# Seven products of quarters for most of a short convolution's input projection

## The chip, the core and the metric

The kernel runs on one core of a Trainium2 chip. The metric is the device time of one execution in microseconds (us). The engines of the core work side by side, each through its own instructions in a fixed order: PE (TensorE: matrix products, with PEld for its weight loads), DVE (VectorE), ACT (ScalarE), POOL (GpSimd), and SP, whose queue issues most DMAs. They wait for each other through semaphores. Matrix products write to PSUM, which holds 8 banks of 128x512 f32; everything else lies in SBUF. POOL works on SBUF alone here.

## What is computed

The kernel computes a whole small decoder: layer 0 with attention, layer 1 with a short convolution, each followed by an MLP and a gated embedding. The change is in the convolution of layer 1, whose reference is:

```python
D_MODEL = 1024; SEQ = 512; CONV_WIDTH = 3
def short_conv(h, w_in, conv_w, w_out):
    D = h.shape[-1]
    proj = h @ w_in
    b_gate = proj[..., :D]
    c_gate = proj[..., D:2 * D]
    u = proj[..., 2 * D:]
    z = c_gate * u
    zc = lax.conv_general_dilated(
        z, conv_w[:, None, :].astype(z.dtype), window_strides=(1,),
        padding=[(CONV_WIDTH - 1, 0)],
        dimension_numbers=('NWC', 'WIO', 'NWC'),
        feature_group_count=D)
    return (b_gate * zc) @ w_out
```

Here `h` is the normed residual stream (512 tokens x 1024 channels) and `w_in` is 1024 x 3072. Everything is f32.

## The kernel before, in words

**Products in three parts.** PE is fed numbers of the type fp32r, which keep fewer bits than f32. So each f32 operand is held as a pair: `hi`, the value cast to fp32r by ACT, and `lo`, the remainder, which DVE (or POOL) computes as `src - hi`. `split` (L218 to L222) issues both: the cast is L221, the subtraction L222. `mm3` (L211 to L217) then makes one product of three matmuls, hi by hi, hi by lo and lo by hi (L213, L214, L215).

**Weights.** All weights are loaded in one planned order, `order`. A weight tile of 128x512 f32 (256 KB) lands in one of 14 `raw` buffers by a DMA of SP's queue (`fetch`, L118), is split into two of the 70 buffers called pages (`prepare`), and is then read by PE. `wide` asks for a tile and has the next 8 of the order prepared with it (`SOON`). In the MLP, which already uses seven products of quarters for its second matrix, `derive` makes four sums of weight quarters per pair on POOL (L130), and POOL also computes the `lo` of those sums (L222 on POOL).

**The convolution** (`conv`). The normed stream lies transposed in `hT` (hi and lo), as 8 blocks of 128 channels by 512 tokens. The three outputs `c`, `u` and `b` are made in blocks of 128 output channels, so 24 blocks in all; `project` makes one block in one PSUM bank: 8 input blocks by three matmuls of 128x512, 24 matmuls. The loop goes over channel pairs `i0 = 0, 2, 4, 6`. For each of the two blocks of a pair it makes c and u, ACT copies c out of PSUM (`cs`, L650), DVE multiplies (`z`, L651), then b is made, and the three taps follow: one product on ACT (L659), two multiply-adds on DVE (L662), the product with b on DVE (L666), and the split into `yh` (ACT) and `yl` (DVE). The first pair is done in halves of 256 tokens, because the last token blocks of `hT` come late from the layer before; its matmuls are 128x256. POOL has no part in the convolution before.

**What follows.** The output product (`co`, in `mixer_out`) sums over all eight `y` blocks for each of 4 token blocks and 2 column halves. It can start with y0 to y5 while the last blocks are finished.

**Order.** The order of instructions on each engine is set when the program is built, by a scheduler that moves instructions on PE, DVE, ACT and POOL by its own estimate of their readiness; on the chip each engine then goes through its list strictly in that order.

Of the kernel before, what the change touches and what calls it, by code (L numbers as in the profile page):

```python
# [15 lines left out]
P = 128  # L16
D = 1024
# [32 lines left out]


class Pair:

# [8 lines left out]
@with_exitstack  # L62
def trunk(ctx: ExitStack, tc, x, pT, g, wv, wqk, bf, wo, wci, cw, wco, wup, wdn, wpp, wpg, out):
    nc = tc.nc
# [9 lines left out]
    def page(name, dtype=F32):  # L74
        return pages.tile([P, S], dtype, tag="pg", name=name)
# [14 lines left out]
    loads, order, where, ready, fetched, begun = [], [], {}, {}, [], [0]  # L90
    derived = {}

    def plan(key, src):
        where[key] = len(order)
        order.append((key, len(loads)))
        loads.append(src)

    def plan_down(l, gr):

        at = {}  # L100
        for name, r, c in (("B11", 0, 0), ("B21", 1, 0), ("B12", 0, 1), ("B22", 1, 1)):
            for p in range(2):
                at[name, p] = len(loads)
                loads.append(wdn[l, c, 4 * gr + 2 * p + r])
        for i in STEPS:
            name = PRODUCTS[i][1]
            for p in range(2):
                where["dn", l, gr, name, p] = len(order)
                order.append((("dn", l, gr, name, p), at if name[0] == "T" else at[name, p]))
        derived[l, gr] = at  # L110

# [7 lines left out]

    def derive(l, gr):  # L120
        at = derived.pop((l, gr))
        fetch(max(at.values()) + 1)
        B = {key: fetched[n][:, :S] for key, n in at.items()}
        for p in range(2):
            for name, a, b in (("T1", "B12", "B11"), ("T3", "B22", "B12"), ("T2", "B22", "T1"),
                               ("T4", "B21", "T2")):
                t = page(f"{name}_{l}_{gr}_{p}")
                derived[l, gr, name, p] = t
                B[name, p] = t[:, :S]
                nc.gpsimd.tensor_tensor(out=B[name, p], in0=B[a, p], in1=B[b, p], op=ALU.subtract)  # L130

    def prepare(upto):
        while begun[0] < min(upto, len(order)):
            n = begun[0]
            begun[0] += 1
            key, at = order[n]
            if key[0] == "dn" and key[1:3] in derived:
                derive(*key[1:3])
# [20 lines left out]
    for l in range(2):  # L159
# [10 lines left out]
        else:  # L170
            for i in range(0, KT, 2):
                for s, key in enumerate((("cu", i), ("b", i), ("cu", i + 1))):
                    for j in range(4):
                        plan((*key, j), wci[3 * (i // 2) + s, j])
            for n in range(2):
# [31 lines left out]
    def need(*keys):  # L207
        while any(k in keys for _, k, _ in later):
            later.pop(0)[2]()
# [420 lines left out]
    def conv(hT):  # L630
# [13 lines left out]

        def gates(i, z, lo, hi):
            n = hi - lo
            c = project(("cu", i), 0, f"c{i}_{lo}", lo, hi)
            u = project(("cu", i), 1, f"u{i}_{lo}", lo, hi)
            cs = page(f"cs{i}_{lo}")
            nc.scalar.copy(cs[:, :n], c[:, :n])  # L650
            nc.vector.tensor_tensor(  # L651
                out=z[:, lo:hi], in0=u[:, :n], in1=cs[:, :n], op=ALU.mult
            )

        def finish(i, z, y, lo, hi):
            n = hi - lo
            b = project(("b", i - i % 2), i % 2, f"b{i}_{lo}", lo, hi)
            a = page(f"za{i}_{lo}")
# [8 lines left out]
            split(y.hi[:, lo:hi], y.lo[:, lo:hi], a[:, :n])  # L667

        for i0 in range(0, KT, 2):
            zs, both = [], []  # L670
            for i in (i0, i0 + 1):
                zs.append(page(f"z{i}"))
                both.append(Pair(page(f"yh{i}", F32R), page(f"yl{i}", F32R)))
            for lo, hi in ((0, 256), (256, 512)) if i0 == 0 else ((0, 512),):
                gates(i0, zs[0], lo, hi)
                finish(i0, zs[0], both[0], lo, hi)
                gates(i0 + 1, zs[1], lo, hi)
                need(*range(NB))
                finish(i0 + 1, zs[1], both[1], lo, hi)
            ys += both  # L680
# [225 lines left out]
def layout(x, p, norm_g, w_attn_in, b_forget, w_attn_out, w_conv_in, conv_w, w_conv_out,  # L906
# [22 lines left out]
    ci = np.stack([c[:, :, 0], u[:, :, 0], b[:, :, 0], b[:, :, 1], c[:, :, 1], u[:, :, 1]], axis=2)  # L929
    got["wci"] = tiles(ci.reshape(D, 3 * D), 2, 256)  # L930
    got["cw"] = np.asarray(conv_w)[0].reshape(3, KT, P).transpose(2, 1, 0)
# [25 lines left out]
```

## Time and profile before

| what | value |
|---|---|
| median of 3 runs | 1249.44 us (1249.13 to 1250.35) |
| the profiled execution's own time | 1248.93 us |
| its span in the trace | 1247.2 us |
| granted clock of PE, mean over the span | 0.998 |
| busy in the span: PE, DVE, ACT, POOL | 1221.6, 918.0, 612.6, 633.9 us |
| convolution, first c matmul to first co matmul | 662.32 to 796.55 us of the span |

A row of a group names the source line, the engine, the operation, the tile written and the tiles read, the shapes and the count; behind the first bar stand the busy time of the group (us) and the mean duration of one (ns); behind the second the idle time of the engine just before, with what ended it. A row of the timeline has the start (us from the span's start), the length (us), the engine, line and operation, and in square brackets the idle time before it. Instructions of one engine overlap a little in the trace: a row of four that lasts 2.49 us has starts 0.62 us apart although one lasts 0.69.

### The profile page before, as it was taken

How to read it: one execution, taken by the hardware profiler on the slowest of the kernel's cores; microseconds unless marked ns; L12 is line 12 of the kernel's file. 1: busy time of each engine (PE TensorE's matmuls, PEld its weight loads, DVE VectorE, ACT ScalarE, POOL GpSimd, SP SyncE). 2: the span in 40 equal slices, each digit the busy share in tenths (PEclk: the TensorE clock that was granted, in tenths of full speed). 3: DMA queues.
4: the chain of work that ended last, by engine and by line, in shares of the span. 5: the costliest groups of instructions: out<-in, count | busy, mean ns of one | idle time of the engine just before them, and what ended most of it. 6: DMA issues, size and time to landing. Idle time of an engine off the chain costs nothing.

```text
span 1247.2 us, 18012 instructions
## 1 busy us (share of the span) xinstructions
PE 1221.6 (98%) x5972; PEld 1023.2 (82%) x5972; DVE 918.0 (74%) x1402; ACT 612.6 (49%) x1309; POOL 633.9 (51%) x631
## 2 busy tenths in 40 slices
PE   7999999999999999999999999999999999999997
PEld 6888887887888888888789888889788888888876
DVE  5657878676789778989877444457778898779972
ACT  5456777546544543454555223333654345535451
POOL 2016667256878777775211000017777778778210
PEclk9999999999999999999999999999999999999999
DMA  7456564532343224428224232432422442236401
GB/s 256 147 159 166 152 157 115 186 116 78 100 135 110 80 82 135 136 74 277 76 83 133 68 100 90 148 119 69 131 63 78 135 135 94 67 110 190 148 18 51
DMA packets 85789, 148.68 MB, mean 119 GB/s; under 512 B 10112, under 2 KB 17328, under 8 KB 85696
## 3 DMA queue, kind: packets, MB, share of 16 engines
q1 hardware_dynamic: 85488, 147.27, 38.2%
q8 instruction: 47, 0.77, 0.3%
q14 instruction: 46, 0.38, 0.1%
q10 hardware_dynamic: 144, 0.26, 0.1%
q0 software_dynamic: 64, 0.00, 0.0%
HBM read 136.93 MB, written 6.37 MB: 115 GB/s over the span
## 4 chain that ended last, share of the span: by engine, by line
PE 69%; DVE 13%; POOL 5%; issue 5%; ACT 4%; DMA 3%; SPq 0%; DVEq 0%; POOLq 0%; ACTq 0%
DVE wl L222 6%; PE up L214 6%; PE up L215 6%; PE up L213 6%; PE dn L214 5%; PE dn L213 5%; PE dn L215 5%; PE pg L213 2%; PE pg L214 2%; PE pg L215 2%; PE qk L214 2%; PE qk L213 2%; PE qk L215 2%; POOL s L715 2%; ACT junk L244 2%
## 5 line engine op out<-in xcount | busy, mean ns | idle before, releaser
L222 DVE TENSOR_TENSOR wl<-raw,wh 128x512 fp32r<-128x512 f32 (+1 forms) x404 | 364.7, 953 | 25.3 <-ACT wh L221 24.3
L221 ACT CAST wh<-raw 128x512 fp32r<-128x512 f32 (+1 forms) x404 | 219.7, 619 | 9.5 <-DVE xd L295 5.0
L214 PE MATMUL up<-hTh,wl 128*128 128x512 f32 (+1 forms) x576 | 210.1, 365 | 0.0
L215 PE MATMUL up<-hTl,wh 128*128 128x512 f32 (+1 forms) x576 | 209.8, 366 | 0.0
L213 PE MATMUL up<-hTh,wh 128*128 128x512 f32 (+1 forms) x576 | 209.3, 366 | 0.0
L222 POOL TENSOR_TENSOR wl<-T,wh 128x512 fp32r<-128x512 f32 x112 | 161.0, 1469 | 35.7 <-ACT wh L221 32.0
L213 PEld LDWEIGHTS up<-hTh,wh 128*128 128x128 f32 x576 | 108.6, 189 | 17.7
L214 PEld LDWEIGHTS up<-hTh,wl 128*128 128x128 f32 x576 | 108.6, 189 | 17.6
L215 PEld LDWEIGHTS up<-hTl,wh 128*128 128x128 f32 x576 | 108.3, 189 | 17.5 <-DVE hTl L222 0.2
L747 DVE TENSOR_TENSOR acc<-dn,acc 128x512 f32<-128x512 f32 x168 | 107.3, 679 | 8.5 <-PE dn L215 8.5
L130 POOL TENSOR_TENSOR T<-raw,raw 128x512 f32<-128x512 f32 x56 | 87.8, 1579 | 36.2 <-DMA raw<-in_wdn 23.7
L701 ACT ACTIVATE r<-up 128x512 f32<-128x512 f32 (+1 forms) x72 | 38.7, 546 | 122.7 <-PE up L215 114.7
L130 POOL TENSOR_TENSOR T<-raw,T 128x512 f32<-128x512 f32 x56 | 90.9, 1623 | 2.2
L687 DVE TENSOR_TENSOR q<-r 128x512 f32<-128x512 f32 (+1 forms) x72 | 68.6, 959 | 28.8 <-ACT r L701 28.6
L236 POOL TENSOR_SCALAR cor_r_v<-cos,cos 128x1 f32<-128x1 f32 x4 | 1.6, 398 | 159.1 <-ACT junk L244 159.1
L221 ACT CAST A11h<-q 128x256 fp32r<-128x256 f32 x28 | 11.4, 407 | 102.0 <-DVE q L687 102.0
L221 ACT CAST wh<-T 128x512 fp32r<-128x512 f32 x112 | 61.2, 617 | 0.0
L213 PE MATMUL pg<-wh,hTh 128*128 128x512 f32 x128 | 50.9, 397 | 3.5 <-ACT hTh L221 3.3
L754 POOL TENSOR_TENSOR acc<-acc,acc 128x512 f32<-128x512 f32 x28 | 46.9, 1706 | 10.1 <-DVE acc L747 10.1
L213 PE MATMUL qk<-hTh,wh 128*128 128x512 f32 x128 | 51.1, 399 | 0.0
L215 PE MATMUL qk<-hTl,wh 128*128 128x512 f32 x128 | 50.9, 397 | 0.0
L214 PE MATMUL pg<-wh,hTl 128*128 128x512 f32 x128 | 50.3, 393 | 0.0
(234 smaller groups left out, 3082.5 us busy)
## 6 DMA issues: line engine op xcount, KB each, us to landing
raw<-in_wup SPq DMA_DIRECT2D x128, 256.0 KB, 2.9
raw<-in_wdn SPq DMA_DIRECT2D x128, 256.0 KB, 2.9
raw<-in_wci SPq DMA_DIRECT2D x48, 256.0 KB, 3.2
raw<-in_wqk SPq DMA_DIRECT2D x32, 256.0 KB, 3.4
raw<-in_wpg SPq DMA_DIRECT2D x32, 256.0 KB, 3.5
g<-in_g SPq DMA_DIRECT2D x22, 256.0 KB, 5.9
prl<-neg_c SPq DMA_DIRECT2D x16, 256.0 KB, 6.6
raw<-in_wo SPq DMA_DIRECT2D x16, 256.0 KB, 5.1
```

The costliest lines, as they stand in the source:

```text
L130: nc.gpsimd.tensor_tensor(out=B[name, p], in0=B[a, p], in1=B[b, p], op=ALU.subtract)
L213: nc.tensor.matmul(ps, a.hi, b.hi, start=start, stop=False)
L214: nc.tensor.matmul(ps, a.lo, b.hi, start=False, stop=False)
L215: nc.tensor.matmul(ps, a.hi, b.lo, start=False, stop=stop)
L221: nc.scalar.copy(hi, src)
L222: eng.tensor_tensor(out=lo, in0=src, in1=hi.bitcast(F32), op=ALU.subtract)
L244: nc.scalar.activation(junk, src, AF.Square, scale=D**-0.5, accum_out=ss)
L687: nc.vector.tensor_tensor(out=out, in0=r, in1=r, op=ALU.mult)
L701: nc.scalar.activation(r[:, :n], ps[:, :n], AF.Relu)
L715: sums = lambda out, a, b, op: nc.gpsimd.tensor_tensor(out=out, in0=a, in1=b, op=op)
L747: nc.vector.tensor_tensor(out=a, in0=banks[s], in1=a, op=ALU.add)
L754: nc.gpsimd.tensor_tensor(out=a, in0=a, in1=acc[i, s][:, :S], op=ALU.add)
```

## The change

For c and b of the channel pairs 2, 4 and 6 and for u of the pairs 4 and 6 (`SEVENS`, eight groups of two output blocks), the product of a 1024 x 256 piece of weights with the 1024 x 512 stream is cut into quarters (512 x 128 of weights, 512 x 256 of the stream) and made by seven products in place of eight, with the scheme that the MLP already uses. The three others (u of pair 2, and all of pair 0) stay as they are.

- The host lays the 36 weight tiles of the pairs 2, 4 and 6 out anew (`wcq`); in a group of seven each of its 4 tiles is one quarter. Their number and size stay.
- `plan_sums` generalizes the plan of the MLP's sums. For each group of seven, POOL makes four sums of quarters (S1, S2, S3, S4). The group then has seven forms to split in place of four: seven casts on ACT, five subtractions on DVE, two (S3 and S4, `ON_POOL`) on POOL.
- `sums_of_tokens` makes four sums T1 to T4 of the stream's quarters, once, for all groups: half of each (q = 0) on DVE, half (q = 1) on POOL, ten 128x512 instructions on each; then eight casts on ACT and eight subtractions on DVE.
- `sevens` makes the seven products: each 4 input blocks by three matmuls of 128x256, two products in one PSUM bank. One ACT copy and seven DVE additions of 128x256, each with one operand in PSUM, put the two output blocks together in two pages in SBUF.
- z and the product with b therefore read SBUF alone where c or b come from sevens. The order within a pair becomes u, c, b for both blocks, and both blocks' taps come after b.

```diff
+SEVENS = {(s, i) for i in (2, 4, 6) for s in "cub" if s != "u" or i > 2}
+QUARTERS = ("A11", "A12", "S2", "S1", "S3", "S4", "A22")
+ON_POOL = ('S3', 'S4')
...
+    def plan_sevens(key, srcs):
+        plan_sums(
+            key,
+            [(f,) for f in QUARTERS],
+            [((name,), src) for name, src in zip(("A11", "A12", "A21", "A22"), srcs)],
+            [
+                ((name,), (a,), (b,), op)
+                for name, a, b, op in (
+                    ("S1", "A21", "A22", ALU.add), ("S2", "S1", "A11", ALU.subtract),
+                    ("S3", "A11", "A21", ALU.subtract), ("S4", "A12", "S2", ALU.subtract),
+                )
+            ],
+        )
...
+    def derive(key):
+        at, sums = recipes.pop(key)
         fetch(max(at.values()) + 1)
+        B = {name: fetched[n][:, :S] for name, n in at.items()}
+        for name, a, b, op in sums:
+            t = page("_".join(str(u) for u in (*key, *name)))
+            derived[(*key, *name)] = t
+            B[name] = t[:, :S]
+            nc.gpsimd.tensor_tensor(out=B[name], in0=B[a], in1=B[b], op=op)
...
-            if isinstance(at, dict):
-                raw, eng, w = derived.pop(key[1:]), nc.gpsimd, S
+            if isinstance(at, tuple):
+                raw, w = derived.pop(key), S
+                eng = nc.gpsimd if key[0] == "dn" or key[-1] in ON_POOL else nc.vector
...
+        def sums_of_tokens():
+            for q, eng in ((0, nc.vector), (1, nc.gpsimd)):
+                cut = lambda h, t: hT.at(
+                    lambda u: u.bitcast(F32)[:, 4 * h + 2 * q : 4 * h + 2 * q + 2, 256 * t : 256 * t + 256]
+                )
+                B = {f"B{h + 1}{t + 1}": cut(h, t) for h in range(2) for t in range(2)}
+                full = {}
+                for name, a, b in (("T1", "B12", "B11"), ("T2", "B22", "T1"),
+                                   ("T3", "B22", "B12"), ("T4", "B21", "T2")):
+                    at = page(f"{name}f{q}")
+                    t = at[:, :S].rearrange("p (k c) -> p k c", k=2)
+                    tt = lambda out, x, y, op: eng.tensor_tensor(out=out, in0=x, in1=y, op=op)
+                    if b in full:
+                        tt(t, B[a].hi, full[b], ALU.subtract)
+                        tt(t, t, B[a].lo, ALU.add)
+                    else:
+                        rest = page(f"{name}r{q}")[:, :S].rearrange("p (k c) -> p k c", k=2)
+                        tt(t, B[a].hi, B[b].hi, ALU.subtract)
+                        tt(rest, B[a].lo, B[b].lo, ALU.subtract)
+                        tt(t, t, rest, ALU.add)
+                    full[name] = t
+                    T[name, q] = Pair(page(f"{name}h{q}", F32R), page(f"{name}l{q}", F32R))
+                    split(T[name, q].hi[:, :S], T[name, q].lo[:, :S], at[:, :S])
...
+        def sevens(key, name):
+            out = [page(f"{name}{e}") for e in range(2)]
+            L, R = slice(0, 256), slice(256, S)
+
+            def products(*pairs):
+                ps = bank(f"{name}_{pairs[0][0]}")
+                for (a, b), c in zip(pairs, (L, R)):
+                    for k in range(4):
+                        w = wide(*key, a).at(lambda u: u[:, k * P : (k + 1) * P])
+                        mm3(ps[:, c], w, second(b, k), k == 0, k == 3)
+                return ps
+
+            add = lambda out, x, y: nc.vector.tensor_tensor(out=out, in0=x, in1=y, op=ALU.add)
+            ps = products(("A11", "B11"), ("A12", "B21"))
+            u = page(f"{name}u")
+            u2, u34 = u[:, L], page(f"{name}v")
+            nc.scalar.copy(u2, ps[:, L])
+            add(out[0][:, L], ps[:, R], u2)
+            p65 = products(("S2", "T2"), ("S1", "T1"))
+            add(u2, p65[:, L], u2)
+            add(u34[:, R], p65[:, R], u2)
+            p73 = products(("S3", "T3"), ("S4", "B22"))
+            add(u34[:, L], p73[:, L], u2)
+            add(out[1][:, R], p65[:, R], u34[:, L])
+            add(out[0][:, R], p73[:, R], u34[:, R])
+            ps = products(("A22", "T4"))
+            add(out[1][:, L], ps[:, L], u34[:, L])
+            return out
...
         for i0 in range(0, KT, 2):
...
+            if i0 == 0:
+                for lo, hi in ((0, 256), (256, 512)):
...
+                        if e:
+                            need(*range(NB))
+                            if lo == 0:
+                                sums_of_tokens()
+                        b = project(("b", 0), e, f"b{e}_{lo}", lo, hi)
+                        taps_of(e, zs[e], both[e], b, lo, hi)
+            else:
+                got = {}
+                for name in "ucb":
+                    if (name, i0) in SEVENS:
+                        got[name] = [o[:, :S] for o in sevens((name, i0), f"{name}{i0}")]
...
+                    if name == "c":
+                        for e in range(2):
+                            times(zs[e][:, :S], got["c"][e], got["u"][e])
+                for e in range(2):
+                    taps_of(i0 + e, zs[e], both[e], got["b"][e], 0, S)
```

`taps_of` is the former `finish` without its `project`; `times` is the DVE product.

More of the change, by code (lines that the diff above doesn't have):

```diff
@@ L62, in trunk @@
 @with_exitstack
-def trunk(ctx: ExitStack, tc, x, pT, g, wv, wqk, bf, wo, wci, cw, wco, wup, wdn, wpp, wpg, out):
+def trunk(ctx: ExitStack, tc, x, pT, g, wv, wqk, bf, wo, wci, wcq, cw, wco, wup, wdn, wpp, wpg, out):
     nc = tc.nc
@@ L643, in project @@
             return ps
-        def gates(i, z, lo, hi):
-            n = hi - lo
[L647 to L657, printed above, removed]
+        T = {}
```

111 lines of the change are left out of this document (72 added, 39 removed).

## The prediction

> **What bounds the kernel now.** I read the page first, then the windows of two stretches, then the groups of each by shape, then the timeline.
>
> ```profile
> span 1247.2 us, 18012 instructions
> ...
> PE 1221.6 (98%) x5972; PEld 1023.2 (82%) x5972; DVE 918.0 (74%) x1402; ACT 612.6 (49%) x1309; POOL 633.9 (51%) x631
> ...
> PEclk9999999999999999999999999999999999999999
> ...
> PE 69%; DVE 13%; POOL 5%; issue 5%; ACT 4%; DMA 3%; SPq 0%; DVEq 0%; POOLq 0%; ACTq 0%
> ```
>
> PE is busy for 98% of the span at full granted clock and holds 69% of the chain of waits. The windows of an MLP stretch and of the convolution's full-width part say how close the others are:
>
> ```profile
> core 0: us, PE busy (x) PEld busy (x) DVE busy (x) ACT busy (x) POOL busy (x), PEclk, DMA share, GB/s
> 400.00:540.00 140.00, 140.00 (x619) 115.92 (x618) 113.08 (x138) 61.34 (x115) 108.69 (x85) 1.00 0.34 104
> 700.00:796.00 96.00, 96.00 (x425) 79.51 (x424) 40.14 (x63) 27.63 (x49) 0.00 (x0) 1.00 0.35 108
> ```
>
> In the convolution PE never pauses, DVE works 42% of the time and POOL not at all. In the MLP, which uses seven products already, DVE stands at 81% and POOL at 78%, and PE still never pauses. So in the convolution a microsecond less of matmuls is a microsecond gained, as long as DVE and POOL keep up.
>
> **What PE gains.** From the timeline, the first matmuls of c and of u in the half-width part, of the first full-width block, and of the output product:
>
> ```profile
> 662.32 0.28 PE L213 MATMUL c<-hTh,wh 128*128 128x256 f32 x1
> ...
> 665.19 0.28 PE L213 MATMUL u<-hTh,wh 128*128 128x256 f32 x1
> ...
> 698.61 0.40 PE L213 MATMUL c<-hTh,wh 128*128 128x512 f32 x1
> ...
> 796.55 0.39 PE L213 MATMUL co<-wh,yh 128*128 128x512 f32 x1
> ```
>
> 24 half-width matmuls take 2.87 us, 0.1196 each. The 18 full-width blocks of the pairs 2, 4 and 6 are 432 matmuls in 97.94 us, 0.2267 each; two halves cost 5% more than a whole. A group of two blocks is 48 x 0.2267 = 10.88 us now and 7 x 4 x 3 = 84 x 0.1196 = 10.05 us after: 0.83 us saved instead of an eighth, and 8 x 0.83 = 6.7 us in all. If PE alone set the pace it would end the convolution at 796.55 - 6.7 = 789.9.
>
> **What the others get.** DVE's prices without POOL (groups by shape, 662 to 800 us), then DVE's and POOL's in the MLP (400 to 540 us):
>
> ```profile
> L222 DVE TENSOR_TENSOR wl<-raw,wh 128x512 fp32r<-128x512 f32 x51 | 32.0, 685 | 0.0
> L651 DVE TENSOR_TENSOR z<-u,cs 128x256 f32<-128x256 f32 x4 | 1.7, 423 | 5.8 <-PE u L215 5.8
> L662 DVE SCALAR_TENSOR_TENSOR za<-z,taps,za 128x256 f32<-128x256 f32 x4 | 1.9, 483 | 1.2 <-ACT za L659 1.2
> ```
>
> ```profile
> L222 DVE TENSOR_TENSOR wl<-raw,wh 128x512 fp32r<-128x512 f32 x46 | 48.7, 1109 | 0.0
> L747 DVE TENSOR_TENSOR acc<-dn,acc 128x512 f32<-128x512 f32 x46 | 29.3, 679 | 1.0 <-PE dn L215 1.0
> L222 POOL TENSOR_TENSOR wl<-T,wh 128x512 fp32r<-128x512 f32 x28 | 41.3, 1505 | 8.8 <-ACT wh L221 7.5 <-PE dn L214 1.3
> L130 POOL TENSOR_TENSOR T<-raw,T 128x512 f32<-128x512 f32 x14 | 22.5, 1607 | 0.5
> ```
>
> The same subtraction of DVE takes 685 ns while POOL is idle and 1109 beside a POOL that is busy 78% of the time; an addition with one operand in PSUM (acc) takes 679 either way. So DVE instructions that read SBUF alone pay 0.42 us each for POOL's company, and those with a PSUM operand nothing. The timeline shows the extreme, both engines with SBUF work queued:
>
> ```profile
> 434.18 5.93 DVE L222 TENSOR_TENSOR wl<-raw,wh 128x512 fp32r<-128x512 f32 x4
> ...
> 430.58 1.33 POOL L130 TENSOR_TENSOR T<-raw,raw 128x512 f32<-128x512 f32 x1 [1.58 <-PE dn L215]
> ...
> 434.43 3.44 POOL L130 TENSOR_TENSOR T<-raw,T 128x512 f32<-128x512 f32 x2
> 437.83 3.44 POOL L130 TENSOR_TENSOR T<-raw,raw 128x512 f32<-128x512 f32 x2
> ```
>
> Here one DVE subtraction takes 1.48 us and one POOL sum 1.72. The Trainium skill, "SBUF — State Buffer", section "Who interferes with whom", has the reason: a DVE instruction with two SBUF inputs and a POOL instruction that reads SBUF exclude each other for the whole instruction. That rule speaks against this change, which gives both of them SBUF work at once; the two rows agree in direction, though 1.48 is less than a full 1.33 on top of 0.62.
>
> The change puts exactly this mix into a stretch where POOL was idle. How DVE goes through a pair today:
>
> ```profile
> 679.27 0.69 DVE L222 TENSOR_TENSOR hTl<-n0b_p,hTh 128x512 fp32r<-128x512 f32 x1 [1.03 <-ACT hTh L221]
> ...
> 760.23 1.54 DVE L662 SCALAR_TENSOR_TENSOR za<-z,taps,za 128x511 f32<-128x511 f32 x2 [0.79 <-ACT za L659]
> 764.11 0.69 DVE L666 TENSOR_TENSOR za<-b,za 128x512 f32<-128x512 f32 x1 [2.35 <-PE b L215]
> 765.55 0.69 DVE L222 TENSOR_TENSOR yl<-za,yh 128x512 fp32r<-128x512 f32 x1 [0.74 <-ACT yh L221]
> 766.16 2.49 DVE L222 TENSOR_TENSOR wl<-raw,wh 128x512 fp32r<-128x512 f32 x4
> ...
> 798.13 0.69 DVE L222 TENSOR_TENSOR yl<-za,yh 128x512 fp32r<-128x512 f32 x1 [0.69 <-ACT yh L221]
> ```
>
> Prices in a queue: an SBUF instruction 2.49 / 4 = 0.62, a multiply-add 1.54 / 2 = 0.77, a half-width addition 0.42, a wait for ACT's cast 0.72 (0.69 and 0.74). With them I go down DVE's built list from the last `hTl`, which ends at 680.0. Charged beside POOL: 0.42 more per SBUF instruction.
>
> - To z of block 1: a half-width `yl`, four weight splits, z: 0.42 + 2.5 + 0.42 = 3.3, to 683.3.
> - Token sums: 10 sums and 8 splits, 18 x 0.62 = 11.2; each of the first four splits waits for ACT's cast, 2.9. POOL makes its own ten sums in the first half, so ten pay the charge, 4.2. 18.3, to 701.6. The four splits of POOL's half stand in DVE's queue, and the rest of pair 0 behind them; PE meanwhile fills PSUM banks with its blocks and has the next two full-width blocks of u to make until 709.5, before it needs a T. I cost this at nothing for PE; without that cover it would be the 3 or 4 us by which T comes after 698.6.
> - Rest of pair 0: 6 multiply-adds of half width at 0.48, 8 others at 0.42, one split, three waits for ACT: 9.1, to 710.7.
> - Pair 2 (c and b by sevens): 11 splits, 2 z, 2 products with b, 2 `yl` = 17 x 0.62, 4 x 0.77, 14 additions x 0.42, two waits: 20.9. All 21 SBUF instructions pay: 8.8. 29.7, to 740.4.
> - Pair 4 (three sevens): 15 splits, so 21 x 0.62, 4 x 0.77, 21 x 0.42, two waits: 26.4; 25 pay: 10.5. 36.9, to 777.3.
> - Pair 6: with two more splits (of the output weights) 27.6. POOL has about 8 of its 18 instructions left, since it works a group ahead; 27 x 0.42 x 8/18 = 5.0. 32.6, to 809.9.
>
> PE needs 3 x 10.05 = 30.2 us for pair 4, and needed 32.7; DVE asks for 36.9. With 18 POOL instructions at about 1.55 us, 28 us, POOL is busy 76% of that, like the 78% behind the charge. So DVE becomes the bound in the pairs 4 and 6, and what goes late is the splits of the next group's weights, which stand between the additions and taps, and at the end `yl` of block 7.
>
> The end: 44 matmuls of the output product stand in PE's built order ahead of the first that reads the last `yl`, 44 x 0.2267 = 10.0 us. PE alone would be there at 789.9 + 10.0 = 799.9, DVE at 809.9. The same place in the number of matmuls is 796.55 + 10.0 = 806.5 now, where nothing waits (last `yl` done at 798.8). So 809.9 - 806.5 = +3.4 us, and everything behind moves by as much.
>
> Costed at nothing: the weight loads, 48 tiles before and after, in groups of four (DMA share 0.35); and ACT, with three casts and a short copy more per group:
>
> ```profile
> L221 ACT CAST wh<-raw 128x512 fp32r<-128x512 f32 x48 | 26.3, 619 | 0.0
> ```
>
> That is some 2.2 us of 10 on an engine that is busy 27.63 of 96; both are covered by waiting that these engines do today. The four quarter sums of the first group (c of pair 2) run on POOL before 680, where DVE still has pauses; if they have none, it is four charges, 1.7 us.
>
> **Sum.** Against the profiled execution's own 1248.93 us (1.7 more than its span, 0.5 under the median): 1248.93 + 3.4 = 1252.3 us.
>
> The charge is the unknown. From 680 on it is paid 10 + 21 + 25 + 12 = 68 times, so DVE ends at 781.3 + 68 x charge. Its bounds are 0 (685 ns without POOL) and 1.48 - 0.62 = 0.86 (the crowded stretch). I take 0.42, the mean of a stretch where POOL is as busy. Up to 0.27 the whole 6.7 us are gained; at 0.37 nothing; at 0.42 it is the forecast.
>
> **Rivals.**
> 1. DVE keeps up, and PE sets the pace: 1248.93 - 6.7 = 1242.2 us. It decides where the charge is under 0.27. For it: additions with a PSUM operand pay nothing, and POOL may mostly find DVE in those, or waiting; half-width additions in a row may cost less than 0.42. Against it: DVE's list for pair 4 is 26.4 of 30.2 us even with no charge, where in the MLP 81% of DVE with the charge in it was enough. Chance 0.30, with parts of the gain.
> 2. POOL paces: a group is 6 x 1.72 = 10.3 us at the crowded price and about 0.6 of waiting for two casts (POOL's splits idle 8.8 us in 28 above), 10.9, the pace of today's group: no gain, about 1249 us. Together with charges around 0.37: 0.20. For it: POOL's queue is a strict one, and its split of S3 waits for a cast that stands behind ACT's copy of the product before. Against it: DVE asks for more.
> 3. Full exclusion: every POOL instruction that meets DVE holds it for its whole 1.33 us. In pair 4 POOL finds 8.8 + 1.4 us of additions and waits, room for 7.7 of its 18; the other 10.3 hold DVE 13.7 us instead of 10.5, a charge of 0.55: DVE ends at 818.7, +12.2, 1261.1 us. Chance 0.13. This is the skill's rule of the section named above, taken literally.
> 4. That sevens are no cheaper on PE is left out: 0.1196 was measured on the same shape with the same streams.
>
> **How the numbers follow.** Forecast 0.37, its own range 1250 to 1257. About 0.2% (2.5 us) is what a measurement of this kernel can tell from no change. Faster 0.30 (rival 1), same 0.20 (rival 2), slower 0.50 (forecast and rival 3). The range that leaves out no more than 2 in 10 has to reach from the full gain, 1242, to the exclusion, 1261.
>
> **What would show it.** Right: in the windows of the pairs 4 and 6 DVE busy over 95%, its weight splits there around 1.1 us, `c`, `b` and `u` matmuls 0.12 us apart with pauses that end on DVE `wl`, and the last `yl` near 810. Wrong: splits under 0.95 us, DVE with pauses that end on PE, and the first `co` matmul near 790. A PE that waits on POOL's `wl` or on ACT casts speaks for rival 2. A pause before the first T product, near 709, would mean that I hid the token sums wrongly.

## The result, and the profile after

| kernel | median (us) | runs | ratio to before, 95% interval |
|---|---|---|---|
| before | 1249.29 (1249.06 to 1250.35) | 4 | |
| after | 1263.14 (1262.76 to 1264.58) | 4 | 1.0111 [1.0096, 1.0126] |

The change costs 13.85 us, 1.1%. Slower was forecast, with 1252.3 us, and the range ended at 1261: the direction was right, the size was wrong by four times. The profiled execution took 1262.76 us. The page of the changed kernel, the lines that answer to those of before:

```profile
span 1261.0 us, 18834 instructions
...
PE 1221.8 (97%) x6260; PEld 1035.6 (82%) x6260; DVE 996.5 (79%) x1484; ACT 629.9 (50%) x1345; POOL 729.0 (58%) x689
...
PE 63%; DVE 18%; issue 6%; ACT 5%; POOL 4%; DMA 2%; SPq 1%; DVEq 0%; POOLq 0%; ACTq 0%
```

DVE has 78.5 us and POOL 95 us more work; PE's busy time is the same to 0.2 us although a group makes seven products in place of eight: the steps at a lower granted clock, shown below, are longer and count as busy. DVE's share of the chain of waits rose from 13% to 18%. PE's timeline bounds the convolution (start, length, engine, line, operation; the split is now L263 and L264, the three matmuls L255 to L257):

```profile
662.53 0.28 PE L255 MATMUL c<-hTh,wh 128*128 128x256 f32 x1
...
809.63 0.40 PE L255 MATMUL co<-wh,yh 128*128 128x512 f32 x1
```

First c to first co is 147.10 us, against 796.55 - 662.32 = 134.23 before: +12.87 of the +13.8 of the span lie here. The windows of that stretch:

```profile
core 0: us, PE busy (x) PEld busy (x) DVE busy (x) ACT busy (x) POOL busy (x), PEclk, DMA share, GB/s
676.00:700.00 24.00, 24.00 (x203) 24.00 (x202) 22.38 (x30) 5.09 (x10) 12.18 (x8) 1.00 0.35 112
700.00:720.00 20.00, 15.76 (x75) 13.02 (x75) 17.30 (x24) 9.65 (x21) 9.55 (x7) 0.91 0.00 0
720.00:730.00 10.00, 10.00 (x86) 10.00 (x85) 9.90 (x14) 4.53 (x9) 9.92 (x7) 1.00 0.34 107
730.00:760.00 30.00, 28.58 (x222) 28.08 (x222) 28.22 (x37) 11.39 (x22) 20.47 (x14) 0.94 0.25 80
760.00:790.00 30.00, 24.78 (x200) 24.34 (x200) 28.28 (x35) 11.45 (x22) 22.54 (x14) 0.93 0.28 88
```

Where PE was busy 96.00 of 96 us at full clock and DVE 40.14, DVE is now busy 95% of the time from 720 to 790 (66.4 of 70 us), PE pauses, and the granted clock falls to 0.91 to 0.94 in three of these windows. The waits of PE and their places in its timeline:

```profile
PE c_A L255 <- ACT wh L263: 6.5, 2, 5.2
PE u L255 <- DVE za L762: 4.2, 1, 4.2
PE c L256 <- DVE wl L264: 1.6, 2, 1.1
```

```profile
706.13 0.39 PE L257 MATMUL u<-hTl,wh 128*128 128x512 f32 x1
710.76 0.66 PE L255 MATMUL u<-hTh,wh 128*128 128x512 f32 x1 [4.24 <-DVE za L762]
711.21 0.63 PE L256 MATMUL u<-hTh,wl 128*128 128x512 f32 x1
```

The same timeline where c of the pairs 4 and 6 is first multiplied with its quarter A12:

```profile
749.50 0.28 PE L257 MATMUL c_A<-hTl,wh 128*128 128x256 f32 x1
751.05 0.38 PE L255 MATMUL c_A<-hTh,wh 128*128 128x256 f32 x1 [1.28 <-ACT wh L263]
...
783.34 0.28 PE L257 MATMUL c_A<-hTl,wh 128*128 128x256 f32 x1
788.84 0.58 PE L255 MATMUL c_A<-hTh,wh 128*128 128x256 f32 x1 [5.22 <-ACT wh L263]
...
790.24 0.41 PE L255 MATMUL c_A<-hTh,wh 128*128 128x256 f32 x1
790.45 0.41 PE L256 MATMUL c_A<-hTh,wl 128*128 128x256 f32 x1
```

After each pause matmuls start 0.43 us apart in place of 0.227 (711.21 on) or 0.21 in place of 0.12 (790.24 on). What the starts of successive matmuls exceed 0.2267 and 0.1196 us by, added up, is 2.2 us at 673 to 681 (the two waits for a `wl` of c), 6.1 at 706 to 714, 3.6 at 749 to 755 and 7.4 at 783 to 793, 19.3 in all. With the 6.4 us that the third experiment shows PE to save, 134.2 - 6.4 + 19.3 = 147.1: PE's account closes.

DVE's account shows why PE waited. Its timeline through the token sums, and then the groups by shape from 720 to 800:

```profile
686.45 0.68 DVE L702 TENSOR_TENSOR T1f<-hTh 128x512 f32<-128x512 f32 x1
...
687.77 1.67 DVE L702 TENSOR_TENSOR T1f<-T1f,T1r 128x512 f32<-128x512 f32 x1
...
691.06 1.78 DVE L702 TENSOR_TENSOR T2f<-hTh,T1f 128x512 f32<-128x512 f32 x1
...
704.80 0.69 DVE L702 TENSOR_TENSOR T4f<-T4f,hTl 128x512 f32<-128x512 f32 x1
...
709.25 0.99 DVE L758 SCALAR_TENSOR_TENSOR za<-z,taps,za 128x255 f32<-128x255 f32 x2
710.28 0.43 DVE L762 TENSOR_TENSOR za<-b,za 128x256 f32<-128x256 f32 x1
```

```profile
L264 DVE TENSOR_TENSOR wl<-raw,wh 128x512 fp32r<-128x512 f32 x20 | 24.8, 1252 | 0.0
L766 DVE TENSOR_TENSOR z<-c,u 128x512 f32<-128x512 f32 x2 | 3.5, 1778 | 0.0
L735 DVE TENSOR_TENSOR b2v<-b_S,b2u 128x256 f32<-128x256 f32 x2 | 0.8, 418 | 0.0
...
L163 POOL TENSOR_TENSOR u_S<-raw,u_S 128x512 f32<-128x512 f32 x2 | 3.5, 1740 | 0.0
L264 POOL TENSOR_TENSOR wl<-c_S,wh 128x512 fp32r<-128x512 f32 x4 | 6.0, 1517 | 17.4 <-ACT wh L263 17.4
```

POOL's half of the token sums runs from 687.51 to 704.2, and its timeline shows the ten back to back:

```profile
687.51 1.37 POOL L702 TENSOR_TENSOR T1f<-hTh 128x512 f32<-128x512 f32 x1 [12.47 <-DVE z L766]
688.85 1.74 POOL L702 TENSOR_TENSOR T1r<-hTl 128x512 f32<-128x512 f32 x1
...
702.59 1.62 POOL L702 TENSOR_TENSOR T4f<-T4f,hTl 128x512 f32<-128x512 f32 x1
```

The same instruction on DVE lasts 0.68 us before POOL starts and after it has ended, and 1.66 to 1.78 between. POOL's own go from 1.37 to between 1.62 and 1.75. The half-width additions with a PSUM operand stay at 0.41 to 0.42 us. What PE waited for at 706 was not a T: it had made the rest of pair 0 and a block of u, and found its next PSUM bank held by the half-width b whose product (L762, done at 710.7) stands in DVE's list behind the token sums.

One window over the rest of DVE's walk, and its waits in it (engine and line that waits, for whom, us in total, times, longest):

```profile
686.40:819.40 133.00, 122.12 (x886) 116.75 (x885) 123.31 (x164) 51.59 (x99) 87.79 (x54) 0.95 0.27 84
```

```profile
DVE yl L264 <- ACT yh L263: 4.7, 7, 0.8
DVE T4l L264 <- ACT T4h L263: 0.7, 1, 0.7
...
DVE za L758 <- ACT za L755: 0.6, 1, 0.6
```

DVE is busy 123.31 of 133 us, and no wait of it listed there is for PE: each is for a cast or tap of ACT that DVE's own result before had released. DVE's last `yl` starts at 818.76 and ends at 819.45; 44 matmuls behind the first co is 809.63 + 10.0 = 819.6. So PE reached the place where it needs the last `yl` just as it was made, and did not wait there. I read this as DVE's list setting the time through the whole stretch, with PE's pauses where the lag happened to show; the experiments test that.

### The profile page after: what moved, and what is told of

Its sections match the earlier page's. It is cut to its first block, busy times and chain, and to the rows that moved or that the text cites. A ratio compares the mean times of both kernels' runs of the same rounds, so it can differ in the third digit from the quotient of the medians.

```text
span 1261.0 us, 18834 instructions
## 1 busy us (share of the span) xinstructions
PE 1221.8 (97%) x6260; PEld 1035.6 (82%) x6260; DVE 996.5 (79%) x1484; ACT 629.9 (50%) x1345; POOL 729.0 (58%) x689
## 4 chain that ended last, share of the span: by engine, by line
PE 63%; DVE 18%; issue 6%; ACT 5%; POOL 4%; DMA 2%; SPq 1%; DVEq 0%; POOLq 0%; ACTq 0%
DVE wl L264 7%; PE up L257 6%; PE up L255 6%; PE up L256 6%; PE dn L256 5%; PE dn L255 5%; PE dn L257 5%; ACT junk L286 2%; PE qk L256 2%; PE qk L255 2%; PE qk L257 2%; DVE n_h L294 2%; POOL s L840 1%; DVE acc L872 1%; PE pg L255 1%
## 5 line engine op out<-in xcount | busy, mean ns | idle before, releaser
L264 DVE TENSOR_TENSOR wl<-raw,wh 128x512 fp32r<-128x512 f32 (+1 forms) x396 | 378.9, 1003 | 24.4 <-ACT wh L263 22.8
L263 ACT CAST wh<-raw 128x512 fp32r<-128x512 f32 (+1 forms) x396 | 216.2, 619 | 9.8 <-DVE xd L337 5.0
L257 PE MATMUL up<-hTl,wh 128*128 128x512 f32 (+1 forms) x576 | 209.7, 366 | 0.3 <-DVE hTl L264 0.3
L255 PE MATMUL up<-hTh,wh 128*128 128x512 f32 (+1 forms) x576 | 209.4, 366 | 0.0
L264 POOL TENSOR_TENSOR wl<-dn_T,wh 128x512 fp32r<-128x512 f32 x112 | 161.0, 1470 | 35.8 <-ACT wh L263 30.4
L257 PEld LDWEIGHTS up<-hTl,wh 128*128 128x128 f32 x576 | 108.3, 189 | 18.0 <-DVE hTl L264 0.5
L255 PEld LDWEIGHTS up<-hTh,wh 128*128 128x128 f32 x576 | 108.6, 189 | 17.5
L163 POOL TENSOR_TENSOR dn_T<-raw,raw 128x512 f32<-128x512 f32 x56 | 89.2, 1605 | 35.2 <-DMA raw<-in_wdn 23.6
L163 POOL TENSOR_TENSOR dn_T<-raw,dn_T 128x512 f32<-128x512 f32 x56 | 90.3, 1612 | 2.2
L263 ACT CAST A11h<-q 128x256 fp32r<-128x256 f32 x28 | 11.4, 406 | 101.5 <-DVE q L812 101.5
L263 ACT CAST wh<-dn_T 128x512 fp32r<-128x512 f32 x112 | 61.2, 617 | 0.0
L255 PE MATMUL pg<-wh,hTh 128*128 128x512 f32 x128 | 50.9, 397 | 3.6 <-ACT hTh L263 3.5
L255 PE MATMUL qk<-hTh,wh 128*128 128x512 f32 x128 | 51.1, 399 | 0.0
L257 PE MATMUL qk<-hTl,wh 128*128 128x512 f32 x128 | 50.9, 397 | 0.0
L256 PE MATMUL qk<-hTh,wl 128*128 128x512 f32 x128 | 50.2, 392 | 0.0
```

The costliest lines, as they stand in the source:

```text
L163: nc.gpsimd.tensor_tensor(out=B[name], in0=B[a], in1=B[b], op=op)
L255: nc.tensor.matmul(ps, a.hi, b.hi, start=start, stop=False)
L256: nc.tensor.matmul(ps, a.lo, b.hi, start=False, stop=False)
L257: nc.tensor.matmul(ps, a.hi, b.lo, start=False, stop=stop)
L263: nc.scalar.copy(hi, src)
L264: eng.tensor_tensor(out=lo, in0=src, in1=hi.bitcast(F32), op=ALU.subtract)
```

## The experiments

Twelve kernels, each timed beside the kernel before on the same chip. "c to co" is first c to first co matmul in the trace of each; before it is 134.23 us.

| experiment | median | before beside it | ratio, 95% interval | c to co |
|---|---|---|---|---|
| 1 the new order alone | 1250.21 | 1249.95 | 0.9998 [0.9988, 1.0007] | 134.24 |
| 2 and the token sums | 1251.99 | 1249.95 | 1.0017 [1.0008, 1.0027] | 136.22 |
| 3 all, POOL writes constants | 1244.66 | 1249.95 | 0.9957 [0.9942, 0.9972] | 127.84 |
| 4 all, token sums later | 1265.16 | 1249.95 | 1.0121 [1.0106, 1.0137] | 149.45 |
| 5 as 3, with the real token sums | 1250.56 | 1250.22 | 1.0002 [0.9992, 1.0012] | 133.51 |
| 6 no remainders on POOL | 1269.13 | 1250.22 | 1.0152 [1.0136, 1.0167] | 153.49 |
| 7 next weights asked for earlier (the lists stay the same) | 1264.36 | 1250.22 | 1.0112 [1.0097, 1.0127] | 147.13 |
| 8 four groups, token sums later | 1247.40 | 1250.22 | 0.9976 [0.9967, 0.9986] | 131.05 |
| 9 five groups, token sums later | 1247.60 | 1250.07 | 0.9979 [0.9970, 0.9988] | 130.60 |
| 10 six groups, token sums later | 1249.04 | 1250.07 | 0.9996 [0.9986, 1.0005] | 131.61 |
| 11 four groups, token sums early | 1249.49 | 1250.07 | 0.9995 [0.9985, 1.0004] | 133.02 |
| 12 all, cast of y on DVE | 1271.19 | 1249.79 | 1.0170 [1.0153, 1.0187] | 156.07 |

The theory was that DVE's list, lengthened by POOL's company, is the bound; the rivals were the token sums by themselves, POOL's pace, and the order of weights and casts.

### 1 and 2: the order, then the token sums, with no group of seven

```diff
-SEVENS = {(s, i) for i in (2, 4, 6) for s in "cub" if s != "u" or i > 2}
+SEVENS = set()
...
-                            if lo == 0:
-                                sums_of_tokens()
```

Experiment 2 has the first edit alone.

> No group of seven and no token sums; what stays is the new order within a pair (u, c, b of both blocks, taps behind b). Theory company (DVE's SBUF instructions beside POOL's are what is too long): 1249 us, within 2 of before, PE without a pause, since POOL is idle. Theory queues (the order in which DVE and ACT go through taps, casts and sums makes PE wait, with or without POOL): some of the loss is here already, 1251 or more, with a pause of PE at a change of pairs.

> No group of seven, but the token sums T1 to T4 are made, half on DVE and half on POOL, and never read. It prices the first pause (4.4 us at 706 us of the changed kernel, and 3.4 us of half clock behind it). If that pause comes from the token sums alone: 1249 + 4.4 + 1.7 = 1255 us, with one pause of PE near 706. If it needs the splits of the sevens' weights too: under 1251.

The order u, c, b and the new layout of the weights cost nothing (134.24 us). The token sums cost 2.0 us of the convolution with nothing else changed, which is between the two times expected, by one wait of PE:

```profile
PE u L255 <- DVE za L762: 1.7, 1, 1.7
```

It is the same wait as in the changed kernel at 706, shorter, and the clock stayed at 1.00 behind it. I had costed this at nothing.

### 3 and 5: the same lists without POOL's reads

```diff
-            nc.gpsimd.tensor_tensor(out=B[name], in0=B[a], in1=B[b], op=op)
+            if key[0] == "dn":
+                nc.gpsimd.tensor_tensor(out=B[name], in0=B[a], in1=B[b], op=op)
+            else:
+                nc.gpsimd.memset(B[name], 0.5)
...
+            if eng is nc.gpsimd and key[0] != "dn":
+                nc.scalar.copy(hi[:, :w], raw[:, :w])
+                nc.gpsimd.memset(lo[:, :w].bitcast(F32), 0.0)
+            else:
+                split(hi[:, :w], lo[:, :w], raw[:, :w], eng)
...
+                    tt = lambda out, x, y, op: (
+                        eng.tensor_tensor(out=out, in0=x, in1=y, op=op) if q == 0 else eng.memset(out, 0.5)
+                    )
```

Experiment 5 has the first two edits, and the token sums as in the change.

> All of the changed kernel, but POOL writes constants where it made quarter sums, the lo of S3 and S4 and its half of the token sums, so it reads nothing in the convolution; the lists of DVE and ACT stay the same but for a few places. Theory company: DVE's splits fall from 1.0 to 1.8 us to about 0.69, its list ends near 782 to 790 us, and PE sets the pace: 1242 to 1246 us. Theory queues: casts still stand behind taps, PE still pauses near the starts of the third groups: over 1252 us.

> As the one without company, but the token sums are real on POOL too; only the groups' quarter sums and the lo of S3 and S4 are constants. It parts the two stretches in which POOL reads: the token sums then cost what e2 showed, about 2 us, so 1244.7 + 2 = 1246 to 1248 us, with at most a pause near 706, if the stretches are independent. If the 4.4 us pause at 706 us belongs to the token sums by themselves, 1244.7 + 6 = 1251.

In experiment 3 nothing is left of the loss: PE has no pause, the clock is 1.00, and the convolution takes 127.84 us, 6.4 less than before. So the scheme's saving on PE is real, 0.8 us a group, and the loss goes with POOL's part. The edit takes away two things at once, POOL's reads of SBUF and the time that POOL's own list needs; that it is the reads rests on the length of DVE's instructions here and on the waits of the changed kernel, none of which, on PE or from 686 us on DVE, ends on POOL. The window of pair 4 and the group of DVE's weight splits:

```profile
751.00:789.00 38.00, 38.00 (x319) 38.00 (x318) 30.68 (x61) 18.11 (x35) 7.13 (x14) 1.00 0.33 94
```

```profile
L271 DVE TENSOR_TENSOR wl<-raw,wh 128x512 fp32r<-128x512 f32 x29 | 19.4, 685 | 5.1 <-ACT wh L270 5.1
```

DVE has nearly the list of the changed kernel here, and room to spare, at 685 ns for a split. POOL only writes here, it reads nothing, and it does not slow DVE. The Trainium skill, "SBUF — State Buffer", section "Who interferes with whom", says just this of an instruction with two SBUF inputs: it contends with a GpSimd instruction that reads SBUF, not with one that only writes it. Trace and rule agree: 685 ns beside POOL's memsets, 1778 beside its sums.

Experiment 5 puts the company back in the token sums alone: 5.9 us over experiment 3 (1250.56 - 1244.66), 5.7 in the convolution, by the wait at 706, 3.9 us, and 3.4 us at half clock behind it. This is the higher of the two times expected, and more than the 2.0 us of experiment 2, where the sums are as real. The traces show a difference: in experiment 2 POOL began its half 10.1 us before DVE did and met only a part of DVE's, in experiment 5 both began 20.5 and 20.6 us after the first c matmul. By subtraction the eight groups' company costs the other 12.6 of 18.5; no run has it alone.

```profile
PE u L262 <- DVE za L769: 3.7, 1, 3.7
```

### 4: the token sums moved to the start of pair 2

```diff
-                            if lo == 0:
-                                sums_of_tokens()
...
                 got = {}
+                if i0 == LATE_AT:
+                    sums_of_tokens()
```

> The token sums are issued behind pair 0 instead of in its middle. Theory company: the same work beside the same POOL, only elsewhere: within 3 us of the changed kernel, 1260 to 1266. Theory queues: the taps of pair 0 no longer wait behind them, PSUM banks come free, the 4.4 us pause and its 1.7 us of half clock go: about 1257, unless the first T product then waits as long.

The wait at 706 is gone, and the time is 2 us longer. Its waits of PE:

```profile
PE c_A L256 <- ACT wh L264: 10.6, 2, 6.4
```

What had been lost at 706 is lost at 746, where the wait is 6.4 us in place of 1.3 at 749, and in a new one of 0.9 at 735; the wait at 786 is 1 us shorter than it was. A list that is too long on DVE isn't made shorter by moving a piece of it: this speaks for DVE as the bound, and against the token sums' place as the cause.

### 6: nothing but the sums on POOL

```diff
-ON_POOL = ('S3', 'S4')
+ON_POOL = ()
```

> DVE makes the lo of S3 and S4 too, POOL only the four sums: 12 POOL instructions fewer per two groups of c, b, u... that is 4 per group in place of 6, and 7 splits on DVE in place of 5. Theory company: each POOL instruction cost DVE about 0.6 us (37.8 us for a pair in place of 26.4, over 18), two fewer save 1.2 per group and two more splits cost 1.24 and their own company: no gain, 1261 to 1267 us. Rival ring (POOL's splits wait 8 to 10 us for ACT's casts and hold up the next sums): that wait goes, 1255 or less.

If POOL had set the pace, taking 16 of its splits would have helped, unless DVE, which gets them, became the bound by it. The time grew by 6 us over the changed kernel's, 2 us past what I had expected at most. So this run alone does not decide; with the waits of the changed kernel, none of which ends on POOL for PE or DVE, rival 2 of the prediction falls.

### 7: the next pair's weights asked for before the taps

```diff
+                if i0 + 2 < KT:
+                    prepare(where["u", i0 + 2, "S1"] + 1)
                 for e in range(2):
                     taps_of(i0 + e, zs[e], both[e], got["b"][e], 0, S)
```

> The first four forms of the next pair's first weights after u's start are asked for ahead of the taps instead of behind them, so that their casts need not wait behind the taps on ACT. Theory company: DVE's list is as long as before and another split is late: within 4 us of the changed kernel, 1259 to 1267. Rival queues: the pauses at 749 and 783 us (7.2 us with their restart, and 4 us of half clock) go: 1252 to 1254.

The same waits of the same length as in the changed kernel, to 0.1 us; the convolution takes 147.13 us. The edit changes nothing: with the eight tiles ahead that `wide` prepares, b's last quarter has already asked for all seven forms of the next u, ahead of the taps. In the two traces each of PE, DVE, ACT and POOL has the same instructions in the same order. So this is the changed kernel a second time, and it decides nothing between the theories.

### 12: is it ACT's list or DVE's?

In the changed kernel the waits at 749 and 783 end on ACT's cast of the A12 weights, which stands in ACT's list behind the cast of y (`yh`). ACT had little to do there, as its timeline shows:

```profile
784.08 0.62 ACT L263 CAST yh<-za 128x512 fp32r<-128x512 f32 x1 [8.82 <-DVE za L762]
...
788.17 0.61 ACT L263 CAST wh<-raw 128x512 fp32r<-128x512 f32 x1
```

It stood 8.82 us behind DVE's taps, with the weight's cast queued behind. The edit takes that cast out of ACT's list:

```diff
-            split(y.hi[:, lo:hi], y.lo[:, lo:hi], a[:, :n])
+            nc.vector.tensor_copy(out=y.hi[:, lo:hi], in_=a[:, :n])
+            nc.vector.tensor_tensor(
+                out=y.lo[:, lo:hi], in0=a[:, :n], in1=y.hi[:, lo:hi].bitcast(F32), op=ALU.subtract
+            )
```

> The full change, with the cast of yh moved from ACT to DVE, where it takes the place of a wait of about as much (0.69 to 0.76 us) for ACT. Both long pauses at c's A12 product end on ACT's cast of the A12 weights, which stands behind the taps' yh in ACT's list. If ACT's list is what holds PE, that cast now runs early, the pauses at 749 and 783 go with their half clock (3.6 and 7.4 us): about 1252 us. If DVE is what holds PE, its own subtraction for the same weights stands behind the taps in DVE's list too and is as late as before: the pause stays within 1 us of its length, and ends on DVE wl instead of ACT wh: 1261 to 1265 us.

Neither number was met. The weights' casts did move ahead, and the kernel became 8 us slower than the changed one. Its waits of PE, and DVE's and POOL's timelines at the taps of pair 4:

```profile
PE c_A L256 <- DVE wl L264: 15.2, 2, 8.4
```

```profile
785.74 3.47 DVE L758 SCALAR_TENSOR_TENSOR za<-z,taps,za 128x511 f32<-128x511 f32 x2
789.24 1.67 DVE L762 TENSOR_TENSOR za<-b,za 128x512 f32<-128x512 f32 x1
790.94 1.38 DVE L763 CAST yh<-za 128x512 fp32r<-128x512 f32 x1
792.36 1.63 DVE L764 TENSOR_TENSOR yl<-za,yh 128x512 fp32r<-128x512 f32 x1
```

```profile
786.92 1.74 POOL L163 TENSOR_TENSOR b_S<-raw,raw 128x512 f32<-128x512 f32 x1
788.74 1.62 POOL L163 TENSOR_TENSOR b_S<-b_S,raw 128x512 f32<-128x512 f32 x1
790.32 1.72 POOL L163 TENSOR_TENSOR b_S<-raw,raw 128x512 f32<-128x512 f32 x1
```

The wait now ends on DVE's subtraction for the same weights: the list that holds PE is DVE's. And it is later than before, because POOL no longer stood 7.99 us at its own split (it waits for a cast too) while DVE did the taps: a product that took 0.69 us in the changed kernel (L762 at 783.28) takes 1.67, a `yl` 1.63. In the changed kernel the blocked cast had kept POOL away from the taps. The casts that DVE took over do not explain it by themselves: away from POOL one lasts 0.43 us (757.22), less than the wait of 0.7 whose place it takes. From the first tap to the last `yl` DVE needs 11.6 us in place of 7.2 in pair 2, and 11.6 in place of 9.2 in pair 4, together 6.8 of the 9.0 us by which the convolution is longer.

### 8 to 11: how many groups DVE can carry

```diff
-SEVENS = {(s, i) for i in (2, 4, 6) for s in "cub" if s != "u" or i > 2}
+SEVENS = {(s, i) for i in (4, 6) for s in 'cb'}
```

This is experiment 8, with the token sums as in experiment 4, so that pair 2 has no group. Experiment 9 adds u of pair 6, experiment 10 u of the pairs 4 and 6; experiment 11 is the four groups with the token sums in pair 0.

> Sevens for c and b of the pairs 4 and 6 alone, token sums behind pair 0. PE saves 4 x 0.83 = 3.3 us, DVE has 22.8 us per pair without and about 31 with company against PE's 31.0: if it just fits, 1249.4 - 3.3 + 2 (token sums) = 1248 us; if the charge is as dear as in the changed kernel's token sums (1.72 us for an instruction), DVE is late by some us per pair: 1252 to 1256.

> Five groups: c and b of pair 4, u, c and b of pair 6; the token sums at the start of pair 2, as in the kernel of four groups. If what counts is whether DVE has room in the pair (my theory: PE pays where DVE's own list of a pair, with the charge for company, is longer than PE's matmuls of it), pair 6 now asks for 15 splits and 21 additions, and PE stands still in it once, 2 to 6 us at the first A12 product of c or u, with a stretch of half clock behind it: 1249 to 1254 us. If instead the number of groups is all that counts, each gives 0.7 to 0.8 us: 1250.2 - 5 x 0.7 = 1246.7 us, no pause.

> Six groups: u, c and b of the pairs 4 and 6; the token sums at the start of pair 2. By my theory both pairs are longer on DVE than on PE (the changed kernel's DVE took 37.8 us for pair 4), but with a whole pair of slack ahead of them, since pair 2 asks for no sevens: one or two pauses of 3 to 6 us, 1251 to 1259 us. If each group gains: 1250.2 - 6 x 0.7 = 1246.0 us.

> The same four groups as the kernel that was faster than before (c and b of the pairs 4 and 6), with the token sums where the change puts them, in pair 0. If the place of the sums costs by itself, as in the kernel with the sums alone (a pause of 1.83 us at u, 1.8 us of time over the order alone): 1247.4 + 1.8 = 1249.2 us, with one pause near 705. If it is the quarter sums' company that makes the token sums costly, and these groups start later, there is nothing more than that; the 4.40 us of the changed kernel's pause with its half clock would give 1253 us or more.

Four groups gain 3.2 us in the convolution, 0.8 each, with no pause of PE and DVE at 65% in pair 4's window:

```profile
735.00:770.00 35.00, 35.00 (x236) 32.41 (x235) 22.91 (x37) 13.78 (x26) 17.42 (x12) 1.00 0.30 91
```

That is the one version with all its work that is clearly ahead of both kernels, if by a quarter of a percent: 0.9976 [0.9967, 0.9986], with experiment 9 equal to it. My theory's figure for five groups (1249 at least) was too high: PE has 0.4 us of extra steps in pair 6 and a wait of 0.9 for `yh` at the output product, no more. The sixth group gives back more than it gains, between the two expectations:

```profile
PE c_A L256 <- ACT wh L264: 1.3, 1, 1.3
PE co L256 <- ACT yh L264: 0.8, 1, 0.8
```

Experiment 11 has the wait of experiment 2 again (1.6 us for `za` L762) and came out at 1249.49, as expected from adding that to the four groups' time. So where DVE has room, the place of the token sums costs 2 us by itself.

## Why the prediction was right or wrong

**PE's saving: right.** 0.83 us a group, 6.7 us, PE alone at 789.9. Experiment 3 measured 6.4 us, and experiment 8 3.2 us for four.

**DVE, not POOL, becomes the bound: right.** It was the step "DVE becomes the bound in the pairs 4 and 6" and the end set by the last `yl`. Experiments 3, 6 and 12 bear it out, and DVE's end of 819.45 less the 10.0 us of cover and less the 796.55 of before gives +12.9, which is what the convolution lost. The rule for the end held in its number, with DVE's end put at 809.9; not as described, for no wait of PE ends on that `yl`. PE lost the time earlier, in waits for a PSUM bank and for weights. The prediction had named a PE that waits on ACT's casts as a sign for rival 2. Such waits came, 6.5 us of them, and did not mean that: those casts stood in ACT's list behind `yh`, which waited for DVE's taps, and experiment 12, which took `yh` out of the way, left PE waiting for DVE's `wl`.

**The sizes of DVE's walk: here it failed.** The stretches, predicted and measured in DVE's timeline. The charge is worked out instruction by instruction, as what each takes above the median of its kind in experiment 3:

| stretch | predicted (us) | measured | charge predicted | charge measured |
|---|---|---|---|---|
| up to the token sums, end | 683.3 | 686.45 | 0 or 1.7 | |
| token sums | 18.3 | 22.8 | 4.2 | 8.7 |
| rest of pair 0 | 9.1 | 11.4 | 0 | 4.0 |
| pair 2 | 29.7 | 30.5 | 8.8 | 10.8 |
| pair 4 | 36.9 | 37.8 | 10.5 | 13.0 |
| pair 6 | 32.6 | 30.5 | 5.0 | 4.5 |
| end | 809.9 | 819.45 | 28.5 | 40.8 |

The failing term is the charge, and its form. I took 0.42 us for every DVE instruction that reads SBUF alone, 68 times. Measured, 47 paid more than 0.2 us, about 0.87 in the mean, which was my upper bound of 0.86 (the crowded stretch), and up to 1.1 each; the others paid little or nothing. In the token sums, where both engines have ten sums queued, seven of DVE's ten sums pay 1.0 to 1.1, three splits about a third of a microsecond, and the first two and the last of the ten nothing: 4.5 us more than charged, all of that stretch's error. The mean of a stretch where POOL is busy 78% of the time was the wrong row for a place where both queue; the crowded row was quoted, and used only for the range. The pairs 2 and 4 came out right within 0.9 us, but that is in part luck. Their charge was 2.0 and 2.5 us too low, and the list without it 1.2 and 1.6 too high: I had priced a half-width addition at the 0.42 us that one lasts, and in a row they start 0.33 apart:

```profile
727.42 0.74 DVE L735 TENSOR_TENSOR c2v<-c_S,c2u 128x256 f32<-128x256 f32 x2
```

Over all stretches the charge was 12.3 us too low, and some 6 of these were made up by prices of this kind: with the right ones, DVE's end would have been put 6 us earlier still.

**Two costs left out.** For the rest of pair 0 I charged nothing. POOL was out of token sums by then, but started the splits and sums of the next groups at 714.5, and the timeline has two half-width `yl` at 1.5 us each. And the sums of c of pair 2 that I put before 680 at "nothing, or 1.7": POOL's four ran from 668.66 to 675.0 and met a queued DVE (four splits in 4.67 us; a queue of four took 2.49 in the profile before), so that PE waited 1.26 and 0.64 us in pair 0, and the token sums began 3.15 us late. With the token sums these make 3.15 + 4.5 + 2.3 = 9.95 us; the three pairs together gave 0.4 back, and 9.55 is what DVE's end was wrong by.

**"I cost this at nothing for PE": wrong, as the sign named for it shows.** A pause near 709 was to mean that the token sums were hidden wrongly; it came at 706, 4.4 us long. I had asked when PE needs a T. PE needed a PSUM bank, which stood behind the token sums in DVE's list. Experiment 2 prices this at 2.0 us of the convolution without the groups, and experiment 5 at 5.7 with the groups' lists on DVE and ACT, where POOL's half of the sums meets DVE's from the start.

**The rivals.** Rival 1 needed a charge under 0.27 and is what experiment 3 shows with no charge at all: 1244.66. Rival 2 is out by experiment 6 and the waits together. Rival 3, full exclusion, gave 1261.1 and was nearest, 2 us under the measured time. Its DVE end, 818.7 against 819.45, is so near by some luck: it has the same too high price of additions in it. I held it at 0.13 because one crowded subtraction took 1.48 us and not 1.33 + 0.62. Measured here, an SBUF sum on DVE takes up to 1.78 us beside a POOL sum of 1.74, and in the token sums the two go one for one. A turn of one on each engine takes about 1.70 us there (DVE's starts 696.17 and 697.87). One after the other, DVE's step alone of 0.60 (706.84 to 707.44) and POOL's shortest sum, 1.30 (668.66), would make 1.90, so exclusion is nearly full, not quite. Its charge of 0.55, worked out by room in the pairs, was still too low for such a place.

**Half clock.** The clock was not in the prediction. It makes 5.1 of PE's 19.3 us (the 17.1 us of 706 to 793 less pauses of 4.4, 1.44 + 0.40 and 5.38 + 0.40). Since DVE's end and PE's arrival fell together within 0.2 us, I take it that at full clock PE would have waited for DVE instead; no run shows the one without the other. In experiment 5, where DVE has room after the token sums, the slow stretch is a loss by itself.

## What to carry to other kernels

When a change gives DVE and GpSimd SBUF work at the same time, price it by how it meets: where both have a queue, a DVE instruction with two SBUF inputs takes a whole turn (here up to 1.1 us more on 0.68, and 0.87 in the mean of those that paid), and a mean from a looser stretch, 0.42, is too low by half. Before a long piece of DVE work is called hidden, look not only at who needs its result but at whose PSUM bank is freed behind it in the list. A scheme that moves work from PE to its helpers has a best dose, here four or five groups of eight with the token sums at the start of pair 2: count the helpers' lists per pair, and stop where they reach PE's.

## What the runs showed of the hardware that I had not expected

**Half clock after short pauses.** The granted clock fell to 0.5 in or behind a pause of PE for 3.41 us or a multiple: 3.41 us from 710.94 (pause 4.40) and from 751.90 (pauses of 1.44 and 0.40 us), 6.83 from 786.04 (pause 5.38), and 10.24 us in experiments 4, 6 and 12 (pauses of 6.57 and 7.04, and of 8.53 and 6.97 in experiment 12). A pause of 1.26 us brought 3.41 us of half clock in experiment 6 and none in the changed kernel; 1.83 us in experiment 2 and 1.44 in experiment 10 brought none. So in these runs the length of one pause does not decide by itself below 2 us. A pause of 1.74 us near 607, which the kernel before has too, was followed by 3.41 us of half clock in experiments 7, 8 and 9 and in none of the other traces. The clock records show what else differs: in every trace the slow stretches within the kernel start a whole number of steps of 3.413 us after its first record at full clock (710.94, 751.90 and 786.04 lie 12 and 10 steps apart). Between 30 and 1235 us, adding up PE's gaps of 0.1 us and more in each step that ran at full clock: none with less than 1.4 us of them was followed by half clock, of those with 1.42 to 1.78 us some were, and of those with 1.87 us or more all. The Trainium skill, "TensorE: Matmul & The Clock Gate", section "What's actually happening", has the half rate come after at least one idle window of about 3.4 us. The length of the steps agrees with that window; the pauses of 1.26 and 1.44 us that were followed by half clock are shorter than it.

**An idle engine's wait can protect another.** In experiment 12 freeing ACT's list let POOL run beside DVE's taps, and the kernel lost 8 us more; the taps of the pairs 2 and 4 alone took 6.8 us longer on DVE.
